# A written order for all engines in the middle of a Strassen MLP, and the first two products of every pair swapped

## Chip, cores and metric

The kernel runs on one core of one Trainium2 chip. The metric is the device time of one execution in microseconds (us), taken as the median of several runs; lower is better.

## What is computed

One layer of a hybrid decoder over 16 meta rows, 1024 prompt rows and 8 x 8 sample rows: two recurrent branches behind one big projection, then a squared-ReLU MLP. What matters here is that nearly all time goes into dense products with 1024-wide activations.

```python
def layer(x, conv_buf, h0, S0, is_prompt, lb, gains, w_in, ...):
    xn = rms_norm(x, gains[0])
    proj = xn @ w_in
...
    mixed = jax.nn.sigmoid(m_a) * (y_a @ w_branch_a) + jax.nn.sigmoid(m_b) * (y_b @ w_branch_b)
    x = x + rms_norm(mixed @ w_out, gains[1])
    hn = rms_norm(x, gains[2])
    ff = jnp.square(jax.nn.relu(hn @ w_up)) @ w_down
    x = x + rms_norm(ff, gains[3])
```

## The kernel before

Every dense product is a 2 x 2 block product in Winograd's form of Strassen's scheme: seven block products in place of eight. A **pair** is one such product: seven weight operands S1, A11, A22, S2, S3, A12, S4 (blocks of the weights and sums of blocks) times seven operands made of the activations. Each operand is held as two f16 tiles, a high part `sh` and a low part `sl`, so that one product is 12 matmuls (4 depth tiles, three combinations of parts, lines 287 to 290). A pair is run twice, once for each half of the columns; one such run of seven products is called a **window** here, c0 and c1 its two columns' halves.

The products of a window accumulate in four PSUM banks b1 to b4. Four products open a bank, three more are added into banks b3, b4 and b1 once the first content has been read out: ACT copies one, DVE adds the next to the copy (that sum is `v`), ACT copies a third (`u`), DVE subtracts. In the kernel before the order is S1 into b4 (ACT copies it, line 1426 in the MLP), S3 into b3 (DVE adds it to v, line 1428), A11 into b1 (ACT copies it, line 1430), S2 into b2 (DVE, line 1432), then A22 onto b3, S4 onto b4, A12 onto b1. So the fifth product, A22, may start only when DVE has read b3 at line 1428.

**Weights of the next pair** are made ready while a pair runs, by the generator `gen_pair` in seven steps (splits): ACT writes `sh` (line 190), DVE writes `sl` (line 191). Sums of blocks are made by DMA: a plain load by SP (line 179) and then an accumulating DMA from the POOL queue onto the same tile `sa` (line 180) give S1; two more accumulating DMAs turn it into S2 (line 222, after the split of S1) and S4 (line 231, after the split of S2). Line 225 turns the tile `ws` with A11 into S3; line 228 (SP) loads A12 over A22; line 161 loads the raw blocks two pairs ahead. There are two `sa` tiles, so the load at line 179 for a later pair waits until S4 of the pair before has been split. The pool `opp` has 11 slots for split operands.

The MLP has 32 pairs: in four groups, four up-projections (`BH`, results squared and split into the f16 tiles `aoh` and `aol` by `up_fin`) and four down-projections (`BA`, results added into `facc` by `dn_fin`). Pairs are numbered 0 to 31 here; pairs 2 to 27 are the **middle**, pairs 0 and 1 (three narrow windows each) the head, pairs 28 to 31 the tail. Before the MLP, the projections and branches use the same scheme through `pair` and `dopair` (line 293).

A scheduler sets the order on each engine from its own estimate of times; each engine then runs its queue strictly in that order. In the MLP TensorE alone runs in the order of the code; ACT, DVE, POOL and SP are in the scheduler's order.

## Time and profile before

| | us |
|---|---|
| median of 3 runs (1943.08 to 1946.82) | 1946.52 |
| the profiled execution | 1943.99 |
| its span, first to last instruction | 1942.2 |
| TensorE busy (92% of the span) | 1782.7 |
| DVE busy (76%) | 1466.5 |
| ACT busy (52%) | 1012.5 |
| middle of the MLP, 1283.2 to 1832.1 | 548.9 |

The span is a chain of stages that TensorE runs through without overlap, so a stage's length and TensorE's waits in it are what counts. Busy shares are averages. Durations of instructions on one engine overlap a little, so the distance between two starts is the time that an instruction costs in a full queue.

### The profile page before, as it was taken

How to read it: one execution, taken by the hardware profiler on the slowest of the kernel's cores; microseconds unless marked ns; L12 is line 12 of the kernel's file. 1: busy time of each engine (PE TensorE's matmuls, PEld its weight loads, DVE VectorE, ACT ScalarE, POOL GpSimd, SP SyncE). 2: the span in 40 equal slices, each digit the busy share in tenths (PEclk: the TensorE clock that was granted, in tenths of full speed). 3: DMA queues.
4: the chain of work that ended last, by engine and by line, in shares of the span. 5: the costliest groups of instructions: out<-in, count | busy, mean ns of one | idle time of the engine just before them, and what ended most of it. 6: DMA issues, size and time to landing. Idle time of an engine off the chain costs nothing. (4 is left out here: it accounts for less than half of the span.)

```text
span 1942.2 us, 43735 instructions
## 1 busy us (share of the span) xinstructions
PE 1782.7 (92%) x17856; PEld 1520.1 (78%) x17856; DVE 1466.5 (76%) x2670; ACT 1012.5 (52%) x2098; POOL 538.3 (28%) x626
## 2 busy tenths in 40 slices
PE   5999999999999999888798898899999889989986
PEld 4888898898878777667677698788888778777776
DVE  7999989788755899877968757976477447645767
ACT  4555555555444787755424344574375236425653
POOL 3511111111222233344623336551211111111132
PEclk9899999999999999989899999999999999999998
DMA  5253332433345444467778632344545445444535
GB/s 178 61 111 84 80 101 68 123 78 90 90 135 146 99 111 111 113 179 223 220 222 241 181 89 70 85 102 105 119 89 114 90 89 101 104 88 100 120 72 162
DMA packets 117337, 230.32 MB, mean 119 GB/s; under 512 B 11152, under 2 KB 45328, under 8 KB 114064
## 3 DMA queue, kind: packets, MB, share of 16 engines
q0 software_dynamic: 45184, 97.28, 25.5%
q1 hardware_dynamic: 62704, 125.24, 20.1%
q10 hardware_dynamic: 9248, 5.02, 1.0%
q8 instruction: 139, 2.28, 0.5%
q14 instruction: 62, 0.51, 0.1%
HBM read 191.43 MB, written 36.06 MB: 117 GB/s over the span
## 5 line engine op out<-in xcount | busy, mean ns | idle before, releaser
L289 PEld LDWEIGHTS <-sh 128*128 128x128 f16 x3920 | 387.5, 99 | 176.5 <-issue 105.7
L287 PEld LDWEIGHTS <-sh 128*128 128x128 f16 x3920 | 388.3, 99 | 79.5 <-issue 4.9
L290 PEld LDWEIGHTS <-sl 128*128 128x128 f16 x3920 | 387.8, 99 | 75.5 <-DVE sl L191 2.3
L287 PE MATMUL q<-aoh,sh 128*128 128x272 f16 (+2 forms) x1008 | 262.5, 270 | 29.5 <-DVE U L1428 26.9
L287 PE MATMUL pd<-tsh,sh 128*128 128x276 f16 (+1 forms) x960 | 272.7, 285 | 13.4 <-DVE gm L347 4.8
L289 PE MATMUL pd<-tsl,sh 128*128 128x276 f16 (+1 forms) x960 | 273.0, 285 | 0.0
L290 PE MATMUL pd<-tsh,sl 128*128 128x276 f16 (+1 forms) x960 | 272.6, 284 | 0.0
L191 DVE SCALAR_TENSOR_TENSOR sl<-sa,sh 128x512 f16<-128x512 f32 x201 | 149.5, 746 | 163.0 <-ACT sh L190 162.8
L287 PE MATMUL q<-hoh,sh 128*128 128x272 f16 (+2 forms) x952 | 256.4, 274 | 12.7 <-DVE U L1428 11.0
L190 ACT ACTIVATE sh<-ws 128x512 f16<-128x512 f32 x288 | 178.6, 626 | 171.3 <-PE q L289 90.1
L290 PE MATMUL q<-aoh,sl 128*128 128x272 f16 (+2 forms) x1008 | 262.5, 270 | 1.8 <-DVE sl L191 1.8
L289 PE MATMUL q<-aol,sh 128*128 128x272 f16 (+2 forms) x1008 | 262.5, 270 | 0.0
L289 PE MATMUL q<-hol,sh 128*128 128x272 f16 (+2 forms) x952 | 256.5, 274 | 0.0
L290 PE MATMUL q<-hoh,sl 128*128 128x272 f16 (+2 forms) x952 | 256.4, 274 | 0.0
L287 PE MATMUL pd<-xh,sh 128*128 128x276 f16 (+1 forms) x776 | 220.0, 283 | 26.0 <-DVE th L341 8.6
L191 DVE SCALAR_TENSOR_TENSOR sl<-ws,sh 128x512 f16<-128x512 f32 x288 | 208.7, 727 | 41.5 <-ACT sh L190 38.8
L190 ACT ACTIVATE sh<-sa 128x512 f16<-128x512 f32 x201 | 125.2, 627 | 202.7 <-DMA sa<-in_w_pr 60.0
L290 PE MATMUL pd<-xh,sl 128*128 128x276 f16 (+1 forms) x776 | 220.3, 284 | 0.0
L289 PE MATMUL pd<-xl,sh 128*128 128x276 f16 (+1 forms) x776 | 220.2, 284 | 0.0
L852 PE MATMUL pd<-sh,xh 128*128 128x128 f16 (+1 forms) x576 | 103.5, 222 | 2.3 <-ACT F L366 2.0
L854 PE MATMUL pd<-sh,xl 128*128 128x128 f16 (+1 forms) x576 | 103.7, 222 | 0.0
L853 PE MATMUL pd<-sl,xh 128*128 128x128 f16 (+1 forms) x576 | 103.5, 222 | 0.0
(332 smaller groups left out, 4234.2 us busy)
## 6 DMA issues: line engine op xcount, KB each, us to landing
sa<-in_w_pr POOLq DMA_DIRECT2D x105, 256.0 KB, 4.2
ws<-in_w_pr SPq DMA_DIRECT2D x35, 512.0 KB, 3.6
sa<-in_w_up POOLq DMA_DIRECT2D x48, 256.0 KB, 4.3
sa<-in_w_dn POOLq DMA_DIRECT2D x48, 256.0 KB, 4.6
sa<-in_w_pr SPq DMA_DIRECT2D x35, 256.0 KB, 3.4
ws<-in_w_pr POOLq DMA_DIRECT2D x35, 256.0 KB, 6.4
ws<-in_w_pr SPq DMA_DIRECT2D x35, 256.0 KB, 4.4
th<-th POOLq DMA_DIRECT2D x16, 544.0 KB, 7.6
```

The costliest lines, as they stand in the source:

```text
L190: ACT.activation(hi, src, AF.Copy, scale=SW)
L191: DVE.scalar_tensor_tensor(lo, src, SW, hi, op0=OP.mult, op1=OP.subtract)
L287: PE.matmul(o, h[:, k, :], bh[:, k, c0:c0 + w], start=first and k == 0, stop=False, skip_group_check=not first)
L289: PE.matmul(o, h[:, k, :], bl[:, k, c0:c0 + w], start=False, stop=False, skip_group_check=not first)
L290: PE.matmul(o, l[:, k, :], bh[:, k, c0:c0 + w], start=False, stop=(k == nk - 1), skip_group_check=not first)
L852: PE.matmul(po, a, wh[:, k % 4, :], start=(k == 0), stop=False)
L853: PE.matmul(po, a, wl[:, k % 4, :], start=False, stop=False)
L854: PE.matmul(po, b, wh[:, k % 4, :], start=False, stop=(k == KT - 1))
```

## The change

Three things change.

- In all pairs the first two products are swapped: S3 into b3 comes first and is the one that ACT copies into v, S1 into b4 comes second and is the one that DVE adds. A22 still goes onto b3 as the fifth product and S4 onto b4 as the sixth.
- In the middle, the order of the code is the order on TensorE, DVE, ACT, POOL and SP (`manual_schedule` over all of them). `up_window` and `dn_window` write it out, product by product. What an up window leaves over (sums of its results and their split into `aoh` and `aol`) is handed on as `rest` and runs behind the first three products of the next window, as `late(0)` to `late(2)`.
- The seven splits of the next pair's weights stand behind fixed products: in c0 behind the second, fourth and sixth, in c1 behind the first, third, fourth and sixth.

In addition the squaring of an up window's results is done in two instructions, and two additions to `facc` in one.

```diff
@@ -291,17 +291,17 @@
                       skip_group_check=not first)
 
     def pair(ops, B, c0, w, s0, s1, tk):
-        t4, t3, t1, t2 = dtags
+        t3, t4, t1, t2 = dtags
         dtags[:] = [t2, t3, t4, t1]
         U = uvp.tile([P, 2, CT], F32, tag="U", name=nm("U"))
         u, v = U[:, 0, :w], U[:, 1, :w]
+        b3 = dtile(t3)[:, :w]
+        prod(b3, ops["S3"], B(5), 4, c0, w, True)
+        ACT.activation(v, b3, AF.Copy)
+        tk(0)
         b4 = dtile(t4)[:, :w]
         prod(b4, ops["S1"], B(3), 4, c0, w, True)
-        ACT.activation(v, b4, AF.Copy)
-        tk(0)
-        b3 = dtile(t3)[:, :w]
-        prod(b3, ops["S3"], B(5), 4, c0, w, True)
-        DVE.tensor_tensor(v, v, b3, op=OP.add)
+        DVE.tensor_tensor(v, v, b4, op=OP.add)
         tk(1)
         b1 = dtile(t1)[:, :w]
         prod(b1, ops["A11"], B(0), 4, c0, w, True)
@@ -1422,10 +1422,10 @@
             if hook:
                 hook(12 * (w / 2400 + 0.0025))
 
+        p(b3, "S3", 5, True)
+        ACT.activation(v, b3[:, :w], AF.Copy)
         p(b4, "S1", 3, True)
-        ACT.activation(v, b4[:, :w], AF.Copy)
-        p(b3, "S3", 5, True)
-        DVE.tensor_tensor(v, v, b3[:, :w], op=OP.add)
+        DVE.tensor_tensor(v, v, b4[:, :w], op=OP.add)
         p(b1, "A11", 0, True)
         ACT.activation(u, b1[:, :w], AF.Copy)
         p(b2, "S2", 4, True)
@@ -1501,19 +1501,130 @@
     facc = fp.tile([P, 2, KT, HW], F32, name="facc")
     mlp["facc"] = facc
 
+
+
+    def up_window(i, ops, c0, w, late, split):
+        b3, b4, b1, b2 = (qbank()[:, :w] for _ in range(4))
+        U = uvp.tile([P, 2, CT], F32, tag="U", name=nm("U"))
+        u, v = U[:, 0, :w], U[:, 1, :w]
+        eb[0] ^= 1
+        e = ep.tile([P, 4, CQ], F32, tag=f"EB{eb[0]}", name=nm("EB"))[:, :, :w]
+        sc = math.sqrt(SA) / KU
+        prod(b3, ops["S3"], BH(5), 4, c0, w, True)
+        ACT.activation(v, b3, AF.Copy)
+        split(0)
+        late(0)
+        prod(b4, ops["S1"], BH(3), 4, c0, w, True)
+        DVE.tensor_tensor(v, v, b4, op=OP.add)
+        late(1)
+        split(1)
+        prod(b1, ops["A11"], BH(0), 4, c0, w, True)
+        ACT.activation(u, b1, AF.Copy)
+        late(2)
+        split(2)
+        prod(b2, ops["S2"], BH(4), 4, c0, w, True)
+        DVE.tensor_tensor(u, b2, u, op=OP.subtract)
+        DVE.tensor_tensor(e[:, 3], u, v, op=OP.subtract)
+        split(3)
+        prod(b3, ops["A22"], BH(6), 4, c0, w, False)
+        DVE.tensor_tensor(e[:, 2], u, b3, op=OP.subtract)
+        ACT.activation(e[:, 2:4], e[:, 2:4], AF.Relu, scale=sc)
+        split(4)
+        prod(b4, ops["S4"], BH(2), 4, c0, w, False)
+        DVE.tensor_tensor(e[:, 0], b4, u, op=OP.subtract)
+        ACT.activation(e[:, 2:4], e[:, 2:4], AF.Square)
+        ACT.activation(e[:, 0], e[:, 0], AF.Relu, scale=sc)
+        split(5)
+        prod(b1, ops["A12"], BH(1), 4, c0, w, False)
+        ACT.activation(e[:, 1], b1, AF.Relu, scale=sc)
+        ACT.activation(e[:, 0:2], e[:, 0:2], AF.Square)
+        split(6)
+        hh, hl_ = aoh[:, :, i, c0:c0 + w], aol[:, :, i, c0:c0 + w]
+        t = [ebuf(n)[:, :544].rearrange("p (s w) -> p s w", s=2)[:, :, :w] for n in range(2)]
+
+        def rest(k):
+            if k == 0:
+                ACT.activation(hh[:, 0:3], e[:, 1:4], AF.Copy)
+                DVE.tensor_tensor(t[0][:, 0], e[:, 1], e[:, 0], op=OP.subtract)
+                DVE.tensor_tensor(t[0][:, 1], e[:, 3], t[0][:, 0], op=OP.add)
+            elif k == 1:
+                ACT.activation(hh[:, 3:5], t[0], AF.Copy)
+                DVE.tensor_tensor(t[1][:, 0], e[:, 3], e[:, 0], op=OP.subtract)
+                DVE.tensor_tensor(t[1][:, 1], t[0][:, 1], e[:, 2], op=OP.subtract)
+                DVE.tensor_tensor(hl_[:, 0:3], e[:, 1:4], hh[:, 0:3], op=OP.subtract)
+            else:
+                ACT.activation(hh[:, 5:7], t[1], AF.Copy)
+                DVE.tensor_tensor(hl_[:, 3:5], t[0], hh[:, 3:5], op=OP.subtract)
+                DVE.tensor_tensor(hl_[:, 5:7], t[1], hh[:, 5:7], op=OP.subtract)
+
+        return rest
+
+    def dn_window(g, o, ops, c0, w, late, split):
...
+        prod(b3, ops["S3"], BA(5), 4, c0, w, True)
+        ACT.activation(v, b3, AF.Copy)
+        split(0)
+        late(0)
+        prod(b4, ops["S1"], BA(3), 4, c0, w, True)
+        DVE.tensor_tensor(v, v, b4, op=OP.add)
+        late(1)
+        split(1)
...
+        if g == 0:
+            DVE.tensor_tensor(f22, u, v, op=OP.subtract)
+        else:
+            DVE.tensor_tensor(f2, f2, u[:, None].to_broadcast([P, 2, w]), op=OP.add)
+            DVE.tensor_tensor(f22, f22, v, op=OP.subtract)
+        split(3)
...
+        return lambda k: None
+
     npair = 8 * NG - 3
-    for q in range(2, npair - 1):
-        g, i = divmod(q, 8)
-        ops = take()
-        for c in range(2):
-            if i < 4:
-                pairc(ops, BH, c * CQ, CQ, up_fin(i))
-            else:
-                pairc(ops, BA, c * CQ, CQ, dn_fin(g, i - 4))
-            if c == 0:
-                wadv(4)
-            else:
-                drain(cur["gen"])
+    PLACES = ((1, 3, 5), (0, 2, 3, 5))
+    with tc.manual_schedule(engines={E.PE, E.DVE, E.Pool, E.Activation, E.SP}):
+        late = lambda k: None
+        for q in range(2, npair - 1):
+            g, i = divmod(q, 8)
+            ops = take()
+            for c in range(2):
+                def split(k):
+                    if k in PLACES[c]:
+                        wadv(1)
+
+                if i < 4:
+                    late = up_window(i, ops, c * CQ, CQ, late, split)
+                else:
+                    late = dn_window(g, i - 4, ops, c * CQ, CQ, late, split)
+            drain(cur["gen"])
+        for k in range(3):
+            late(k)
     hctx.close()
     l1 = sbuf(ctx, "l1", 21)
     l2 = sbuf(ctx, "l2", 2)
```

POOL's queue at pairs 12 and 13 (both down) before: each DMA from this queue stands here with its line; the `sa` and `ws` numbers tell the pairs' tiles apart.

```order
L222 DMA sa_20630<-in_w_dn 128x512
L180 DMA sa_20880<-in_w_dn 128x512
L225 DMA ws_20511<-in_w_dn 128x512
L231 DMA sa_20630<-in_w_dn 128x512
L180 DMA sa_21117<-in_w_dn 128x512
L222 DMA sa_20880<-in_w_dn 128x512
L225 DMA ws_20774<-in_w_dn 128x512
L231 DMA sa_20880<-in_w_dn 128x512
```

The same place in the changed kernel:

```order
L180 DMA sa_20822<-in_w_dn 128x512
L222 DMA sa_20558<-in_w_dn 128x512
L225 DMA ws_20468<-in_w_dn 128x512
L231 DMA sa_20558<-in_w_dn 128x512
L180 DMA sa_21060<-in_w_dn 128x512
L222 DMA sa_20822<-in_w_dn 128x512
L225 DMA ws_20733<-in_w_dn 128x512
L231 DMA sa_20822<-in_w_dn 128x512
```

Before, L222 of one pair stands ahead of L180 of the next pair's sum at pair 12 and behind it at pair 13; now it stands behind it at every pair of the middle.

ACT's queue over the two windows of pair 13 before (L1426 copies v, L1430 copies u, L190 is a split):

```order
L190 ACTIVATE sh_21120<-sa_20880 128x512
L190 ACTIVATE sh_21125<-ws_20774 128x512
L190 ACTIVATE sh_21130<-ws_20774 128x512
L190 ACTIVATE sh_21135<-sa_20880 128x512
L1426 ACTIVATE U_21021<-q_21017 128x272
L1430 ACTIVATE U_21021<-q_21019 128x272
L190 ACTIVATE sh_21240<-ws_20774 128x512
L1426 ACTIVATE U_21144<-q_21140 128x272
L190 ACTIVATE sh_21244<-ws_20774 128x512
L190 ACTIVATE sh_21250<-sa_20880 128x512
L1430 ACTIVATE U_21144<-q_21142 128x272
```

The same windows in the changed kernel (L1569 copies v, L1577 copies u):

```order
L1569 ACTIVATE U_21033<-q_21029 128x272
L190 ACTIVATE sh_21063<-sa_20822 128x512
L1577 ACTIVATE U_21033<-q_21031 128x272
L190 ACTIVATE sh_21096<-ws_20733 128x512
L190 ACTIVATE sh_21128<-ws_20733 128x512
L1569 ACTIVATE U_21150<-q_21146 128x272
L190 ACTIVATE sh_21164<-sa_20822 128x512
L1577 ACTIVATE U_21150<-q_21148 128x272
L190 ACTIVATE sh_21195<-ws_20733 128x512
L190 ACTIVATE sh_21214<-ws_20733 128x512
L190 ACTIVATE sh_21247<-sa_20822 128x512
```

Before, four splits stood in a row, the fourth of them S2, ahead of the copy of v in c0; now the copy of v is ahead, S1 follows it, and S2 comes in c1 behind that window's copy of v.

DVE's queue in c1 of pair 10 (up) in the changed kernel, from the split of S2 on (L1518 adds the second product to v, L1526 reads the fourth, L1548 to L1558 are what the window before left over, L191 is a split):

```order
L191 SCALAR_TENSOR_TENSOR sl_20406<-sa_20028,sh_20405 128x512
L1548 TENSOR_TENSOR ET_20384<-EB_20259 128x272
L1549 TENSOR_TENSOR ET_20384<-EB_20259,ET_20384 128x272
L1518 TENSOR_TENSOR U_20390<-U_20390,q_20387 128x272
L1552 TENSOR_TENSOR ET_20385<-EB_20259 128x272
L1553 TENSOR_TENSOR ET_20385<-ET_20384,EB_20259 128x272
L1554 TENSOR_TENSOR aol<-EB_20259,aoh 128x3x272
L1557 TENSOR_TENSOR aol<-ET_20384,aoh 128x2x272
L1558 TENSOR_TENSOR aol<-ET_20385,aoh 128x2x272
L191 SCALAR_TENSOR_TENSOR sl_20447<-ws_19938,sh_20446 128x512
L1526 TENSOR_TENSOR U_20390<-q_20389,U_20390 128x272
```

The same window before (L1428 adds to v, L1432 reads the fourth product, L1281 and L1288 are leftovers):

```order
L191 SCALAR_TENSOR_TENSOR sl_20504<-ws_19985,sh_20503 128x512
L1428 TENSOR_TENSOR U_20394<-U_20394,q_20391 128x272
L1281 TENSOR_TENSOR ET_20356<-ET_20355,EB_20347 128x272
L1288 TENSOR_TENSOR aol<-EB_20347,aoh 128x3x272
L191 SCALAR_TENSOR_TENSOR sl_20508<-ws_19985,sh_20507 128x512
L1288 TENSOR_TENSOR aol<-ET_20355,aoh 128x2x272
L191 SCALAR_TENSOR_TENSOR sl_20514<-sa_20104,sh_20513 128x512
L1288 TENSOR_TENSOR aol<-ET_20356,aoh 128x2x272
L1432 TENSOR_TENSOR U_20394<-q_20393,U_20394 128x272
L191 SCALAR_TENSOR_TENSOR sl_20634<-sa_20367,sh_20633 128x512
L191 SCALAR_TENSOR_TENSOR sl_20639<-ws_20248,sh_20638 128x512
```

Before, S1 and A11 of the pair after next (`sl_20634`, `sl_20639`) were already split in this window; now the window splits S2, S3, A12 and S4 of the next pair, and the split of S2 stands ahead of the leftovers and of the addition to v.

## Rows read from the trace of the kernel before

**Rows 1.** The page's first lines: span, and TensorE's busy time.
```profile
span 1942.2 us, 43735 instructions
PE 1782.7 (92%) x17856; PEld 1520.1 (78%) x17856; DVE 1466.5 (76%) x2670; ACT 1012.5 (52%) x2098; POOL 538.3 (28%) x626
```

**Rows 2.** Busy time by stage: us, PE, PEld, DVE, ACT, POOL (count), clock, DMA, GB/s.
```profile
90.00:1120.00 1030.00, 964.89 (x9635) 812.15 (x9633) 852.59 (x1361) 563.44 (x1138) 284.87 (x328) 0.98 0.50 134
1283.20:1832.10 548.90, 520.22 (x4372) 432.49 (x4369) 342.87 (x708) 264.90 (x498) 95.83 (x114) 0.98 0.47 102
1832.10:1928.10 96.00, 84.63 (x1050) 76.68 (x1047) 67.78 (x171) 46.94 (x118) 25.83 (x23) 1.00 0.52 130
```

**Rows 3.** The same view: five undisturbed pairs, and the time after a wait.
```profile
1344.00:1440.00 96.00, 96.00 (x831) 81.04 (x829) 52.63 (x103) 42.81 (x82) 15.95 (x19) 1.00 0.50 106
1510.50:1514.00 3.50, 3.50 (x18) 2.35 (x16) 1.92 (x5) 0.00 (x0) 0.40 (x1) 0.51 0.44 75
```

**Rows 4.** TensorE's waits in the middle, 1283.2 to 1832.1: total us, times, longest.
```profile
PE q L287 <- DVE U L1428: 28.6, 17, 3.6
```

**Rows 5.** Timeline at pair 13: start, duration, engine, line; in brackets idle before, releaser.
```profile
1500.25 0.86 POOL L180 DMA_DIRECT2D sa<-in_w_dn  x1 [13.54 <-DVE facc L1473]
1500.79 1.22 POOL L222 DMA_DIRECT2D sa<-in_w_dn  x1
...
1508.39 0.63 ACT L190 ACTIVATE sh<-sa 128x512 f16<-128x512 f32 x1 [8.11 <-DMA sa<-in_w_dn]
1508.93 0.38 ACT L1426 ACTIVATE U<-q 128x272 f32<-128x272 f32 x1
...
1509.05 0.69 DVE L191 SCALAR_TENSOR_TENSOR sl<-sa,sh 128x512 f16<-128x512 f32 x1 [7.17 <-ACT sh L190]
...
1510.14 0.28 PE L287 MATMUL q<-aoh,sh 128*128 128x272 f16 x1 [3.46 <-DVE U L1428]
```

**Rows 6.** Timeline at pair 11, where L222 stands ahead of L180.
```profile
1459.75 0.86 POOL L222 DMA_DIRECT2D sa<-in_w_dn  x1 [13.79 <-DVE sl L191]
1462.28 0.86 POOL L180 DMA_DIRECT2D sa<-in_w_dn  x1 [1.66 <-DMA sa<-in_w_dn]
...
1463.50 0.63 ACT L190 ACTIVATE sh<-sa 128x512 f16<-128x512 f32 x1 [1.73 <-DMA sa<-in_w_dn]
```

**Rows 7.** Timeline at the end of pair 13: DVE's split of S4, SP's load, POOL's sum.
```profile
1520.90 0.69 DVE L191 SCALAR_TENSOR_TENSOR sl<-sa,sh 128x512 f16<-128x512 f32 x1 [0.65 <-ACT sh L190]
...
1521.62 0.38 SPq L179 DMA_DIRECT2D sa<-in_w_up  x1
...
1525.40 0.86 POOL L180 DMA_DIRECT2D sa<-in_w_up  x1 [14.49 <-DVE sl L191]
```

**Rows 8.** Timeline of DVE in c1 of pair 10, a full queue.
```profile
1455.03 1.00 DVE L1288 TENSOR_TENSOR aol<-EB,aoh 128x816 f16<-128x816 f32 x1
1455.95 0.69 DVE L191 SCALAR_TENSOR_TENSOR sl<-ws,sh 128x512 f16<-128x512 f32 x1
1456.55 0.72 DVE L1288 TENSOR_TENSOR aol<-ET,aoh 128x544 f16<-128x544 f32 x1
...
1458.42 0.44 DVE L1432 TENSOR_TENSOR U<-q,U 128x272 f32<-128x272 f32 x1
1458.77 0.69 DVE L191 SCALAR_TENSOR_TENSOR sl<-sa,sh 128x512 f16<-128x512 f32 x1
```

**Rows 9.** Groups of instructions: an up window's first squaring step, busy us, mean ns, idle.
```profile
L1447 ACT ACTIVATE EB<-EB 128x544 f32<-128x544 f32 (+2 forms) x34 | 21.4, 630 | 35.6 <-DVE EB L1446 35.5
```

**Rows 10.** TensorE's waits before 1130, in the head, and in the tail.
```profile
PE pd L287 <- DVE U L304: 15.1, 9, 6.8
...
PE q L287 <- DVE U L1428: 2.2, 3, 1.5
...
PE q L287 <- DVE U L1428: 7.0, 6, 2.5
PE q L287 <- ACT sh L190: 2.6, 2, 1.6
```

30 lines of the change are left out of this document (added).

## The prediction

> **What bounds the kernel now.** I read the page first, then busy time by stage, TensorE's waits by stage, and last the timelines of one bad and one good pair. TensorE is busy for 1782.7 us of a span of 1942.2 [rows 1], and its stages follow one another, so the question is what it waits for in each. The middle of the MLP is 548.9 us long [rows 2]. It holds 26 pairs of 168 matmuls, 4368 in all. In five pairs that nothing disturbs, 829 matmuls take 96.00 us [rows 3], which is 0.1158 us each, 1.39 us for a product of 12, 9.73 us for a window and 19.46 us for a pair. So 4368 matmuls need 505.8 us, and 43.1 us of the middle are lost. The one wait that the trace lists there is on the addition to v at line 1428: 28.6 us in 17 waits, the longest 3.6 [rows 4]. The rest is what follows the long ones: right after the 3.46 us wait of pair 13 the granted clock is 0.51, which is the 1.2 GHz level, for some 3.5 us [rows 3, 5], and 18 matmuls take the time of 30.
>
> The bad pair shows the mechanism [rows 5]. POOL issues L180, the sum for a later pair, and 0.54 us behind it L222, which turns S1 into S2. ACT's next instruction is the split of S2; it sits idle for 8.11 us until that DMA has landed. Behind it in ACT's queue stands the copy of v, behind that on DVE the split's second half and the addition to v, and TensorE's fifth product waits for that addition. In the good pair [rows 6] L222 goes first, is split 3.75 us after its issue, and L180 follows.
>
> **The change, part by part.**
>
> *The written order, copies of v.* In c0 the copy of v now stands ahead of any split, and S2's split has moved to c1, behind the copy of v there. So a late L222 no longer holds up the fifth product: with the swap that product needs only ACT's copy of the first one, and it has three products, 4.2 us, for that. The addition to v is now needed by the sixth product. The chain of [rows 5] (split of S2, copy, addition, product) is cut in all 26 pairs. What it cost was 43.1 us.
>
> *What is late next: the loop through POOL.* L180 now stands ahead of L222 everywhere. L180 waits for SP's load, and that load waits until S4 of the pair before has been split, since there are two `sa` tiles. That closes a loop: load, L180, L222, split of S2, split of S4, next load. Its parts:
> - From the end of S4's split at 1521.59 the load follows at once and L180 3.78 us after the load's issue [rows 7]: 3.8 us.
> - From L180's issue to L222's data. Lower bound: one such DMA alone takes 3.75 us [rows 6], and L222 is issued about 0.9 later, so 4.6. Upper bound: 8.1 us, where three DMAs went off together [rows 5]. The two behind the first cost (8.1 - 3.75) / 2 = 2.2 us each; in the new order the third, L225, waits for the split of A11, two products later. I take 3.75 + 2.2 = 5.9 us.
> - The split of S2 on ACT and DVE, 0.63 + 0.69 and the handover [rows 5]: 1.4 us.
> - From there to the end of S4's split. In an up window DVE's queue holds five sums at 0.35 us, a split of the window's results at 0.92, two at 0.63, the splits of S3 and A12 at 0.60 each and four more sums at 0.35 [rows 8]: 6.5 us; the last of them feeds ACT, which has three steps of squaring, two of them at 0.63 [rows 9] and a shorter one, some 1.4 us, before S4's split, 1.3 us. That makes 9.1 us with a little overlap. In a down window there is little between, and the limit is L231, 0.3 + 3.75, and S4's split, 1.3: 5.4 us.
>
> The loop is 3.8 + 5.9 + 1.4 + 9.1 = 20.2 us in an up pair and 16.5 in a down pair, against TensorE's 19.46. Up pairs fall back by 0.7 us each, down pairs win up to 3.0 back. Falling back costs nothing at first. ACT reaches S2's split about 11.7 us into the pair in any case; in the first up pair after down pairs L180 is issued at about 4.0 and L222 lands at 9.9, so 1.8 us are free. From the second up pair on, S4 having been split at 22.2, L180 comes at 22.2 + 3.8 - 19.46 = 6.5, L222's data at 12.4, then 0.7 later in each pair: 13.1, 13.8. The first product of the next pair needs S3, whose split ends 4.6 us behind that of S2, at 11.7 + 1.4 + 4.6 = 17.7: 1.8 us of room. The fourth up pair uses up 2.1 of it. So each of the three groups of four up pairs ends with a few tenths of waiting. I book 4 us for this and for handovers, 39 us of gain for the middle. No wait stays above 2 us, so I expect no fall of the clock.
>
> Here the notes have another price. The Trainium skill, "DMA: Bandwidth & Descriptors", section "Anatomy of one DMA — SWDGE (gpsimd) path", gives a POOL-issued DMA as a fixed 2.0 us plus its bytes over 436 GB/s, for 256 KB an estimate of 2.6 us; [rows 6] has 3.75 alone. By the page the loop of an up pair would be under 19.46, none of the 4 us would be left, and the forecast would be 1896.
>
> *DVE's and ACT's load.* An up window costs DVE nine sums at 0.35, one at 0.92, two at 0.63 and 3.5 splits at 0.60 [rows 8]: 7.4 of 9.73 us. It is not the bound while it doesn't stand waiting for S2 for more than 2.3 us a window. The split in two squarings is a fraction of a microsecond on ACT, which is half idle (264.90 of 548.9 [rows 2]); no cost.
>
> *The swap outside the middle.* Before 1130 us TensorE waits 15.1 us in 9 waits for the same addition, line 304, the longest 6.8 [rows 10]. The swap gives each one product, 1.4 us, of air: at most 6 waits of under 1.4 in full, and 1.4 from the longer, 8.5 us in all. The scheduler also lays out this part anew from its own estimates, which moves splits and sums past each other on every queue; nothing in the trace of before prices that, so from 8.5 gained to 8 lost, and I take 3 gained. In the head there are 2.2 us in 3 waits, I take 2. In the tail 7.0 us in 6 waits, of which about 5 can go; but S3, the fifth split, is now needed by the first product instead of the second, and the two waits on splits, 2.6 us [rows 10], can each grow by 1.4. I take 2, from 5 gained to 3 lost.
>
> Sum: 39 + 3 + 2 + 2 = 46. The profiled execution took 1943.99 us (span 1942.2), 2.5 under the median; 1943.99 - 46 = 1898, beside the median 1900.5. **I forecast 1900 us.**
>
> **Rivals.**
>
> *The loop is slower than I took it (R1).* If L222 lands 8.1 us behind L180, as at pair 13, the loop of an up pair is 22.4 us, 2.9 over TensorE's. In a group the first up pair is free, the second waits 1.5, the third and fourth 2.9 each, the first down pair 1.6: 8.9, three groups, and 3 for pairs 2 and 3: 28 us left in the middle. Gain 15 + 7, time 1925. For it: that is what the trace measures with this very order of the queue. Against: there three transfers and an SP load went off together; the new places spread them.
>
> *The loop holds every pair (R2), the case on the slow side.* If the DMAs from POOL slow down beside a DVE that never rests, the same loop decides everything from about 9.6 us between L180 and L222's data: then up pairs lose 4.4 us each (14 of them, 62 us less 12 of room) and down pairs, 3.8 + 9.6 + 1.4 + 5.4 = 20.2, start to lose too, and the 50 us of waits in middle and swap are eaten. At 10.5 us it is 63 for up and 20 for down pairs, 1946.5 + 83 - 50 = 1980. Against it: L222 at 1459.75 was issued just behind a stretch in which DVE ran without a gap [rows 8] and took 3.75 us all the same [rows 6]. This is where a rule of the notes speaks against the change: the Trainium skill, "SBUF — State Buffer", section "SBUF: two separate sides", has POOL-issued DMAs starve for descriptors while DVE runs an operation in a two-port mode. The rows named show no sign of it.
>
> *The swap does harm where the scheduler lays out anew (R3).* The middle gains 39, the first 1130 us lose 8 and the tail 3, the head gains 2: 1946.5 - 30 = 1916.
>
> *Nothing changes (R4):* the copy of v waits elsewhere, for instance behind squarings that wait for DVE. ACT's queue ahead of the copy of v then holds S4's split and two squarings, done about 2 us into the pair; the copy is needed at 5.6. I give it 0.02, 1946.
>
> **How the numbers follow.** Forecast 0.65, R1 0.17, R3 0.12, R4 0.02, R2 0.04. The low end takes all of the 43, 8.5 before, 2 in the head and 5 in the tail: 1946.5 - 58.5 = 1888, and I go to 1887. The high end reaches over R3 and to R1's 1925: 1926. Left out are R2, R4 and part of R1. Faster by more than 0.2% (3.9 us, about what a measurement of this kernel can tell from no change) in all but R2 and R4 and a little of R1: 0.94; within 0.2%: 0.02; slower: 0.04.
>
> **What would show it.** In the profile after: the middle between 506 and 515 us long; no wait of TensorE on the line that adds to v above 1 us and none on the fifth product; the granted clock 1.00 throughout the middle; L180 ahead of L222 on POOL with 5 to 7 us from L180's issue to the split of S2; ACT's waits for `sa` 1 to 2 us, growing from the second to the fourth up pair. R1 would show TensorE waiting at the sixth product of c1 or the first of the next pair, in up groups, by 1.5 to 3 us; R2 in down pairs as well. R3 would show in the first 1130 us alone. I am wrong about the mechanism if ACT no longer waits for S2 and TensorE still waits at the fifth product.

## The result, and the profile after

The changed kernel takes 1928.13 us (median of 4 runs, 1922.59 to 1928.96), the kernel before, timed beside it, 1945.80 (1943.08 to 1946.82): a ratio of 0.9907, with a 95% interval of 0.988 to 0.9934. It is faster, as forecast, by 17.7 us instead of 46; 1928 lies 2 us above the range. The profiled execution took 1927.69.

By stage, from the two traces (a stage begins with TensorE's first product in it):

| stage | before | after | difference | forecast |
|---|---|---|---|---|
| ahead of the MLP's head (start of head) | 1231.1 | 1248.2 | +17.1 | -3 |
| head | 52.1 | 51.4 | -0.7 | -2 |
| middle | 548.9 | 513.7 | -35.2 | -39 |
| tail | 96.0 | 98.4 | +2.4 | -2 |

The page's first lines (span; busy time) stand beside [rows 1]: TensorE has as much to do as before, and the span is 16.3 us shorter.

```profile
span 1925.9 us, 43547 instructions
PE 1780.8 (92%) x17856; PEld 1519.6 (79%) x17856; DVE 1472.3 (76%) x2654; ACT 1013.9 (53%) x2126; POOL 558.4 (29%) x626
```

**The middle did what it should.** Busy time by stage, columns as in [rows 2], and all of TensorE's waits in the middle, as in [rows 4]:

```profile
1299.61:1813.35 513.74, 508.12 (x4372) 426.86 (x4370) 342.44 (x687) 263.33 (x523) 95.64 (x114) 1.00 0.49 107
```

```profile
PE q L287 <- DVE U L1518: 3.6, 7, 0.8
PE q L290 <- DVE sl L191: 2.0, 6, 0.3
```

The 28.6 us in 17 waits of [rows 4] have become 3.6 in 7, none over 0.8, all at the sixth product and none at the fifth. The granted clock is 1.00 where it was 0.98. Against 505.8 us without any stall, 7.9 are left.

**The loss is ahead of the MLP, and in one place.** Ahead of the MLP a trace holds 70 windows of 84 matmuls. The products u and g and gates 3 to 7, beside which the chain of the RG-LRU runs on ACT, DVE and POOL, are windows 28 to 53 (counted from 0). The first five of them lose nothing (52.9 us before, 52.2 after), so I cut at the first matmul of windows 33 and 53, and "the section" means that stretch from here on. Ahead of it (the heads and these five windows) the changed kernel is 4.9 us shorter, behind it 2.2. The section itself, before and after:

```profile
656.13:915.60 259.47, 230.61 (x1808) 180.28 (x1806) 228.69 (x315) 176.59 (x301) 103.89 (x114) 0.96 0.54 141
```

```profile
650.64:934.89 284.25, 236.70 (x1808) 182.42 (x1806) 231.71 (x315) 178.16 (x301) 115.81 (x114) 0.93 0.49 130
```

The same 1808 matmuls take 24.8 us more, at a granted clock of 0.93 instead of 0.96. TensorE's waits there, before and after (lines 300, 304 and 308: copy of v, addition to v, copy of u):

```profile
PE pd L287 <- DVE th L341: 8.6, 3, 5.5
PE pd L287 <- DVE gm L347: 4.8, 4, 2.5
...
PE pd L287 <- DVE U L304: 2.4, 2, 1.8
...
PE pd L287 <- ACT U L308: 1.6, 2, 1.0
```

```profile
PE pd L287 <- ACT U L308: 19.5, 8, 3.9
PE pd L287 <- ACT th L405: 7.9, 2, 7.5
PE pd L287 <- DVE U L304: 6.0, 2, 3.3
PE pd L287 <- DVE th L347: 4.3, 1, 4.3
```

The copy of u is not a line that the diff touches. Five of its eight waits stand some 29 us apart, each at A12 in the first half of a pair (2.5, 3.9, 2.9, 3.7, 2.5 us, together 15.4). They stand in windows 36 to 44; at window 35 the delay is 0.3 us, at window 45 it is 19.4 (counting 84 matmuls to a window), so most of the loss is made there. This is ACT's queue at the second of them, and TensorE behind it:

```profile
719.83 0.38 ACT L300 ACTIVATE U<-pd 128x276 f32<-128x276 f32 x1
...
724.40 1.32 ACT L1068 ACTIVATE th<-th,sm 128x1128 f32<-128x1128 f32 x1
725.62 0.65 ACT L381 ACTIVATE et<-gm 128x552 f32<-128x552 f32 x1
726.29 1.28 ACT L1071 ACT_TABLE_LOAD   x1
727.59 1.14 ACT L1071 ACTIVATE th<-th 128x1128 f32<-128x1128 f32 x1
...
731.22 1.31 ACT L1032 ACTIVATE uc<-up,par,cwk 128x1128 f32<-128x1128 f32 x1
732.44 0.21 ACT L1038 ACTIVATE convout<-up 128x24 f32<-128x24 f32 x1
732.56 0.38 ACT L308 ACTIVATE U<-pd 128x276 f32<-128x276 f32 x1
```

```profile
728.70 0.28 PE L289 MATMUL pd<-xl,sh 128*128 128x276 f16 x1
728.82 0.28 PE L290 MATMUL pd<-xh,sl 128*128 128x276 f16 x1
732.99 0.39 PE L287 MATMUL pd<-xh,sh 128*128 128x276 f16 x1 [3.89 <-ACT U L308]
733.17 0.44 PE L289 MATMUL pd<-xl,sh 128*128 128x276 f16 x1
733.40 0.44 PE L290 MATMUL pd<-xh,sl 128*128 128x276 f16 x1
```

Between the copies of v and u ACT works through 12 us of the RG-LRU, of results and of splits, with a single gap of 0.51 us. TensorE waits 3.89 us, and afterwards its matmuls come 0.23 us apart instead of 0.12, at a granted clock of 0.50 (the third number from the end of this row), the 1.2 GHz level, as after the wait in [rows 5]:

```profile
733.00:736.50 3.50, 3.01 (x13) 1.84 (x13) 3.50 (x4) 0.40 (x1) 0.00 (x0) 0.50 0.34 61
```

Why does the copy of u hurt now? The scheduler sets TensorE's order here too, and the order in which it let the products of one pair begin has changed (p, a, b: second half of the previous pair, first and second half of this one; shown are windows 39 to 41):

```
before   a.S1 a.A11 p.S3 a.S2 a.S4 a.A12 p.A22 | b.S1 b.S2 b.A11 a.S3 b.S4 b.A12 (a.A22 follows)
after    a.S3 a.S2 p.S1 a.S1 a.A22 p.S4 a.S4 a.A11 a.A12 | b.S2 b.S3 b.A11 b.A22 b.A12 (b.S1 follows)
```

Before, in windows 37 to 45, every half leaves S3 and A22 over for the next half, A11 comes early, and at least two products, mostly three in a first half, lie between A11 and A12, in which ACT copies u. After, first halves leave nothing over and A11 stands directly ahead of A12 on the same bank: TensorE has to stand still until u is copied. From window 48 on neither kernel carries anything over. What makes the scheduler do this is what most of the experiments are about.

### The profile page after: what moved, and what is told of

Its sections match the earlier page's. It is cut to its first block, busy times and chain, and to the rows that moved or that the text cites. A ratio compares the mean times of both kernels' runs of the same rounds, so it can differ in the third digit from the quotient of the medians.

```text
span 1925.9 us, 43547 instructions
## 1 busy us (share of the span) xinstructions
PE 1780.8 (92%) x17856; PEld 1519.6 (79%) x17856; DVE 1472.3 (76%) x2654; ACT 1013.9 (53%) x2126; POOL 558.4 (29%) x626
## 5 line engine op out<-in xcount | busy, mean ns | idle before, releaser
L191 DVE SCALAR_TENSOR_TENSOR sl<-ws,sh 128x512 f16<-128x512 f32 x288 | 210.2, 733 | 63.3 <-ACT sh L190 62.6
L287 PE MATMUL pd<-xh,sh 128*128 128x276 f16 (+1 forms) x776 | 222.3, 287 | 36.2 <-ACT U L308 19.5
L191 DVE SCALAR_TENSOR_TENSOR sl<-sa,sh 128x512 f16<-128x512 f32 x201 | 151.1, 754 | 133.0 <-ACT sh L190 131.8
L190 ACT ACTIVATE sh<-ws 128x512 f16<-128x512 f32 x288 | 173.8, 622 | 92.5 <-PE pd L289 63.3
L190 ACT ACTIVATE sh<-sa 128x512 f16<-128x512 f32 x201 | 124.7, 623 | 124.3 <-DMA sa<-in_w_pr 57.1
```

The costliest lines, as they stand in the source:

```text
L190: ACT.activation(hi, src, AF.Copy, scale=SW)
L191: DVE.scalar_tensor_tensor(lo, src, SW, hi, op0=OP.mult, op1=OP.subtract)
L287: PE.matmul(o, h[:, k, :], bh[:, k, c0:c0 + w], start=first and k == 0, stop=False, skip_group_check=not first)
```

## The experiments

### Is it the swap in `pair`, and where?

Four kernels: `pair` put back, the rest as changed (e1); `pair` swapped in the kernel before (e2); the swap only in the RG-LRU section (e3); everywhere but there (e4), the last two by a switch around the first two products that is set ahead of window 28 and behind window 53.

```diff
@@ pair (e1: as before; e2: the reverse, in the kernel before; e3, e4: chosen by section)
-        t3, t4, t1, t2 = dtags
+        t4, t3, t1, t2 = dtags
-        prod(b3, ops["S3"], B(5), 4, c0, w, True)
-        ACT.activation(v, b3, AF.Copy)
+        prod(b4, ops["S1"], B(3), 4, c0, w, True)
+        ACT.activation(v, b4, AF.Copy)
...
```

> The changed kernel with only the helper `pair` put back (S1 first, S3 second, as in the kernel before); the written middle and the swap in `pairc` stay. In the trace of the changed kernel the last product ahead of the MLP ends 15 us later than before (1134.3 against 1119.3) and the MLP's head starts 17.1 us later, while the middle is 35.2 us shorter. Theory A, the swap in `pair` makes that loss by itself: the last product ahead of the MLP goes back to 1119 to 1121, the middle keeps its 513.7, and the time is 1928 - 17 = 1911 (1908 to 1914). Rival B, the written middle changes what the scheduler does ahead of it, so that the loss is not the swap's: the end ahead of the MLP stays at about 1134 and the time at 1928.

> The kernel before with nothing changed but `pair` (S3 first, S1 second); the MLP is as it was. Theory A: the last product ahead of the MLP at about 1134 instead of 1119, and 1946 + 17 = 1963 (1959 to 1966). Rival B (the loss comes with the written middle): 1943 to 1946, the end ahead of the MLP at 1116 to 1120. The prediction's own step said 1943.

> The changed kernel with the swap in `pair` only from the RG-LRU section on (the u and g products and gates 3 to 7) up to the start of the y products; the heads and gates 0 to 2, and the y products, run in the old order. In the trace of the changed kernel the lead over the kernel before is 4.8 us at window 33 (the heads gain a little) and turns to a delay of about 19 us by window 49. Theory A1, the loss is made where it shows, in the RG-LRU section: no gain in the heads, the same delay of 20 to 24 us in the section, and 1911 + 22 = 1933 (1928 to 1938). Rival A2, the loss is handed over by what the swap does earlier, in the heads (a background that is left over, a rotated buffer): no delay here, 1908 to 1914.

> The mirror of the run with the swap in the RG-LRU section only: the swap in `pair` everywhere but there. Theory A1 (the loss is made in the RG-LRU section): the heads keep their gain of 2 to 5 us, the section costs nothing, and the time is 1928 - 22 = 1906 (1903 to 1911). Rival A2 (the loss is handed over from the heads): the end ahead of the MLP stays near 1134 and the time at 1924 to 1930.

| kernel | median us | ratio to before (95%) | RG-LRU section us |
|---|---|---|---|
| e1, `pair` as before | 1913.42 | 0.9831 (0.9814 to 0.9849) | 260.1 |
| e2, only `pair` swapped | 1962.70 | 1.0090 (1.0068 to 1.0111) | 284.1 |
| e3, swap in the section only | 1935.67 | 0.9948 (0.9933 to 0.9964) | 284.4 |
| e4, swap everywhere but there | 1900.05 | 0.9764 (0.9740 to 0.9788) | 259.7 |

All four came out as theory A and A1 had it (e4 3 us better than its range): the written middle has no part in the loss, the swap makes it by itself, and all of it in the RG-LRU section, by 24.1 to 24.6 us in each pair of kernels. Outside the section the swap gains a little. Everything else from the first window to the MLP's head takes 871.5 to 880.3 us in the 16 kernels with the swap or one of its variants (below) there, and 880.8, 888.3, 880.5 and 881.0 in the four without: 8 us by the means, 6 if the 888.3 of e1 is left out. By the medians e4 is 13.4 us faster than e1, and the changed kernel 7.5 faster than e3, so the size of this gain is known only roughly. How far single executions scatter shows e1, whose products ahead of the MLP end 5.5 us later than before (1124.8 against 1119.3) with the instructions of all engines in the very same order up to there; so a difference of a few us in one place of one trace says nothing, and only the 20 and more in the section do.

### What about the swap does it?

First, three guesses that fell or said little, each on the changed kernel or on e4 (whose section is in the old order). The mirror image, S1 first but S4 fifth and A22 sixth (e8, in the section alone; e12, everywhere ahead of the MLP); u copied by DVE (e9); six splits instead of four in a pair's first half (e10).

```diff
@@ pair, in the section (e8) or everywhere (e12), with S1 first
-        prod(b3, ops["A22"], B(6), 4, c0, w, False)
-        s1.both(c0, w, (u, b3), (u, v))
         prod(b4, ops["S4"], B(2), 4, c0, w, False)
         s0.one(1, c0, w, b4, u)
+        prod(b3, ops["A22"], B(6), 4, c0, w, False)
+        s1.both(c0, w, (u, b3), (u, v))
@@ pair, in the section (e9)
-        ACT.activation(u, b1, AF.Copy)
+        DVE.tensor_copy(u, b1)
@@ dopair, in the section (e10)
-                if (c == 0 and i in (1, 2, 4, 6)) or c == 1:
+                if (c == 0 and i in (0, 1, 2, 4, 5, 6)) or c == 1:
```

> The same base, but in the RG-LRU section the mirror image of the swap: S1 first and S3 second as in the kernel before, and instead of them the fifth and the sixth product change places (S4 fifth, on the bank that ACT copied; A22 sixth, on the bank that DVE added). The fifth product gets the same extra time between its bank's last reader and its first matmul as in the changed kernel, without S3's weights coming first. Theory H (that the extra time makes the scheduler lay the section out anew, and the new layout is the loss): the section costs 15 to 25 us, time 1915 to 1925. Rival I (what costs is S3 as first product, whose weights are the fifth of seven splits): section at most 4 us, time 1898 to 1904.

> The changed kernel with `pair` as the mirror image everywhere ahead of the MLP: S1 first and S3 second as before, S4 fifth and A22 sixth. With `pair` as before everywhere the time is 1913, with the swap outside the RG-LRU section and the old order or the mirror within it 1900. Theory O (the 13 us between these come from the extra time that the fifth product gets outside the section, and the mirror gives the same): 1897 to 1904. Rival P (they come from the order of S3 and S1, or from a chance layout): 1909 to 1917.

> The changed kernel with one edit: in the RG-LRU section the copy of u (line 300 plus 8 of the changed kernel, ACT, 0.38 us) is done by DVE. In the trace of the changed kernel TensorE waits 21.4 us in 9 places for that copy, which stands on ACT behind the RG-LRU's exponential, table loads, square root and convolution. Theory J (that place in ACT's queue is the loss): the waits go, the section loses 16 to 22 us less, time 1906 to 1913. Rival K (the queues are full in these stretches, and the wait moves to the next evacuation on ACT or onto DVE): time 1920 to 1932.

> The changed kernel, and in the RG-LRU section the splits of the next pair's weights stand earlier in the code: six in a pair's first half, behind every product but the fourth, instead of four, so that S3's split (the fifth) stands two products earlier. Theory M (the section loses because S3, the first product now, has its weights so late that the scheduler plans the pair late and puts other work of ACT and DVE ahead of it): the section loses at most 12 instead of 24.8, time 1905 to 1916. Rival N (the place of S3's split is not the reason): 1922 to 1934.

e8 took 1900.31 us (0.9774, 0.9753 to 0.9794), section 258.6; e12 1900.74 (0.9759, 0.9735 to 0.9784), section 257.9. Rival I and theory O hold by their numbers, but the mirror is a weaker test than I meant it to be: in the section the scheduler gives it the same order of products as the kernel before, since it leaves S3 and A22 over in any case (windows 36 to 44 are in the very same order). e9 took 1927.32 (0.9911, 0.9881 to 0.9942), section 287.3, and the wait moved to DVE, as rival K said:

```profile
PE pd L287 <- DVE U L311: 21.4, 6, 5.7
```

Line 311 is that kernel's copy of u. So neither ACT nor DVE, both with full queues, copies u in time. e10 took 1927.11 (0.9902, 0.9873 to 0.9932), section 284.6: rival N, moving S3's split two products ahead does not help, and TensorE's order of products in windows 36 to 44 stays that of the changed kernel.

Next, the order of products and the banks. S3 first with S4 fifth (e13). Changed kernel with A22 and S4 held back until A11 has been issued (e16). The line that hands the banks on, changed so that A11 takes over the first product's bank (e14, changed kernel) or the second's (e15, S1 first, on e4).

```diff
@@ pair, e14 everywhere; e15 in the section, in its branch with S1 first
-        dtags[:] = [t2, t3, t4, t1]
+        dtags[:] = [t2, t4, t3, t1]
@@ pair, in the section (e16); the same for S4
-        prod(b3, ops["A22"], B(6), 4, c0, w, False)
+        with tc.issue_after(a11.ins):
+            prod(b3, ops["A22"], B(6), 4, c0, w, False)
```

> The kernel with the swap in `pair` everywhere but in the RG-LRU section (1900 us), and in that section S3 first and S1 second as in the changed kernel, but S4 fifth and A22 sixth, so that the fifth product stands on the bank that DVE adds, without extra time. It is the fourth case of the section: S1 first with A22 fifth 0 us, S3 first with A22 fifth +24.8, S1 first with S4 fifth about -0.5, and this one. Theory I (S3 ahead of S1 is what costs): +18 to +30, time 1918 to 1930. Rival L (only S3 first together with the extra time costs, because then the addition of v may come late): 0 to 6, time 1898 to 1906.

> The changed kernel with one order forced in the RG-LRU section: TensorE may issue a pair's fifth and sixth products (A22, S4) only behind its A11, so that A11 and A12 are never neighbours. Banks and everything else stay. Theory S (the neighbourhood of A11 and A12, with the copy of u between them, is the loss): the five waits of together 15.4 us go, time 1908 to 1917. Rival T (A11 stands late because its bank is late; forced ahead, TensorE waits for the bank instead): 1922 to 1936.

> The changed kernel with one line of `pair` changed, the one that hands the four PSUM banks on to the next half: t3 and t4 change places in it, so that A11 of the next half takes over the bank of the first product (now S3's, finished fifth) instead of the second's (now S1's, finished sixth), as it does in the kernel before by product slot. In the changed kernel's instructions the scheduler has put A11 directly ahead of A12, on the same bank, in the first half of five u pairs; A12 then has to wait for ACT's copy of u, and the five long waits for that copy (2.5, 3.9, 2.9, 3.7, 2.5 us, together 15.4) are at these places. Theory Q (the bank that A11 takes over is released too late, so the scheduler defers A11): the section loses at most 10 instead of 24.8 us, time 1905 to 1914. Rival R (A11 is deferred for another reason, or the loss comes from the gates): 1922 to 1934.

> The kernel with the swap in `pair` everywhere but in the RG-LRU section (1900 us), which has S1 first there; in that section the banks are handed on with t3 and t4 exchanged, so that A11 takes over the bank of the second product (here S3's). It is the reverse of the run that changes the hand-over in the changed kernel. Theory Q (what costs is that A11 inherits the bank of the second product): the section costs 8 to 25 us, time 1908 to 1925. Rival U (only S3 first costs, whichever way the banks go): 1896 to 1904.

| kernel | median us | ratio to before (95%) | section us |
|---|---|---|---|
| e13, S3 first, S4 fifth | 1931.48 | 0.9920 (0.9893 to 0.9946) | 286.1 |
| e16, A11 held ahead of A22 and S4 | 1928.24 | 0.9917 (0.9892 to 0.9942) | 287.2 |
| e14, S3 first, banks handed on otherwise | 1921.66 | 0.9866 (0.9832 to 0.9899) | 280.7 |
| e15, S1 first, banks handed on otherwise | 1922.78 | 0.9873 (0.9838 to 0.9908) | 279.6 |

e13 is theory I's (1.5 us above its range): the extra time for the fifth product doesn't matter, though here too the scheduler gives windows 36 to 44 the changed kernel's order. e16 is rival T's. In the first halves A11 and A12 now stand two products apart, and TensorE waits less for the copy of u (its line 311, beside 19.5 us and 3.9 above), but more for two of DVE's instructions (lines 315 and 406; 0.3 and 1.0 us for the same two in the changed kernel):

```profile
PE pd L287 <- ACT U L311: 10.9, 7, 2.2
...
PE pd L287 <- DVE U L315: 7.6, 6, 1.7
PE pd L287 <- DVE up L406: 7.5, 5, 3.4
```

The same time is lost in other waits, so the neighbourhood looks like the form of the loss and not its cause. That is not settled: the forced order is a new layout with waits of its own, and in most of the second halves a single product stands between A11 and A12, as in the changed kernel. In each of the slow orders of this study some window from 36 to 44 has one product or none between the two, in the fast ones never fewer than two. e14 missed both ranges (theory Q by 8 us, the rival by less than one): the section is 3.5 us shorter, and still 21 too long. e15 fits theory Q: with S1 first, and nothing but another hand-over of banks, the section loses 20 us. What e14 and e15 share is in the order of products: neither carries any product from one half into the next within the section.

That left the roles: who is copied into v and who is added to it. Two kernels cross them with the written order. e20 has S1 first and the old banks, but v begins with S3; e22 has S3 written first, but v begins with S1, and each product is on its old bank.

```diff
@@ pair, e20 (against the kernel before)
         prod(b4, ops["S1"], B(3), 4, c0, w, True)
-        ACT.activation(v, b4, AF.Copy)
         tk(0)
         prod(b3, ops["S3"], B(5), 4, c0, w, True)
-        DVE.tensor_tensor(v, v, b3, op=OP.add)
+        ACT.activation(v, b3, AF.Copy)
+        DVE.tensor_tensor(v, v, b4, op=OP.add)
@@ pair, e22 (against the changed kernel)
-        dtags[:] = [t2, t3, t4, t1]
+        dtags[:] = [t3, t2, t4, t1]
         prod(b3, ops["S3"], B(5), 4, c0, w, True)
-        ACT.activation(v, b3, AF.Copy)
         tk(0)
         prod(b4, ops["S1"], B(3), 4, c0, w, True)
-        DVE.tensor_tensor(v, v, b4, op=OP.add)
+        ACT.activation(v, b4, AF.Copy)
+        DVE.tensor_tensor(v, v, b3, op=OP.add)
```

> The changed kernel with `pair` as in the kernel before in the order of its products (S1 first) and in its banks; of the swap it keeps only the roles of the two evacuations: ACT copies S3's bank into v, DVE then adds S1's. Theory X (the loss comes from v starting with S3, whose weights come late in the row of splits: S1's bank can't be let go before S3's copy, while in the kernel before S1 is copied at once and S3 with its bank may run one half late): the RG-LRU section costs 18 to 28 us though S1 is first, time 1918 to 1932. Rival Y (the order in which the two products are written costs): section 0 to 5, time 1896 to 1908.

> The converse: the changed kernel with S3 written first and S1 second in `pair`, but with the roles as in the kernel before (ACT copies S1's bank, DVE adds S3's) and each product on the bank that it has there (S3's bank stays S3's from half to half). Theory X: the section costs at most 5 us, time 1896 to 1908. Rival Y (S3 written first costs): section 18 to 28 us, time 1918 to 1932.

e20 took 1928.44 us (0.9927, 0.9908 to 0.9947), e22 1903.13 (0.9801, 0.9770 to 0.9833). The section's row of e20 and then of e22:

```profile
650.18:939.19 289.01, 236.22 (x1808) 181.92 (x1806) 227.38 (x315) 177.97 (x302) 122.36 (x114) 0.94 0.49 130
```

```profile
653.62:913.05 259.43, 227.11 (x1809) 178.22 (x1806) 227.29 (x311) 175.04 (x299) 104.35 (x113) 0.97 0.52 138
```

Theory X holds both ways: 289.0 us with S1 first, 259.4 with S3 written first (e20's loss in the section, 29.5 us, is 1.5 above its range). The products of one pair, as laid out:

```
e20      a.S1 p.S3 a.S2 p.A22 p.S4 a.S3 a.A11 a.A22 a.A12 a.S4 | b.S1 b.S2 b.A11 b.A12 (b.S3, b.A22, b.S4 follow)
e22      a.S1 a.A11 p.S3 a.S2 a.S4 a.A12 p.A22 | b.S1 b.S2 b.A11 a.S3 b.S4 b.A12 (a.A22 follows)
```

e22, with S3 first in the code, has the order of the kernel before in these windows. e20 carries three products over and is slow all the same, so carrying alone is not what makes the old layout fast. Over all 20 traces: ten kernels in which v begins with S1 and the banks go as before have sections of 257.6 to 261.9 us; ten in which either is changed have 279.6 to 289.0, and none lies between. These are not twenty cases: in windows 36 to 44 there are only eight orders of products. Nine of the fast ten share that of the kernel before (e22 has one of its own), and five of the slow ten share that of the changed kernel. The crossing of roles, banks and written order rests on one kernel each: e20, e15 and e22.

### What carries the middle, and what is left in it?

e6 is e4 with S1 first and copied in the written middle; e7 is the kernel before with only `pairc` swapped; e5 is e4 with L222 ahead of L180 on POOL in the middle; e17 is e12 with S2's split one place later.

```diff
@@ up_window, dn_window (e6); the reverse in pairc of the kernel before (e7)
-        prod(b3, ops["S3"], BH(5), 4, c0, w, True)
-        ACT.activation(v, b3, AF.Copy)
+        prod(b4, ops["S1"], BH(3), 4, c0, w, True)
+        ACT.activation(v, b4, AF.Copy)
...
@@ sum_load and gen_pair, in the middle (e5)
-            nc.gpsimd.dma_start(q, src[:, 1], accum_op=OP.add)
...
             nc.gpsimd.dma_start(q, src[:, 2], accum_op=OP.add)
+            nc.gpsimd.dma_start(q2, src2[:, 1], accum_op=OP.add)
@@ the middle (e17)
-    PLACES = ((1, 3, 5), (0, 2, 3, 5))
+    PLACES = ((1, 3, 5), (1, 2, 3, 5))
```

> The same base (swap in `pair` everywhere but in the RG-LRU section), and in the written middle alone the first two products in the old order: S1 first and copied by ACT, S3 second and added by DVE, the fifth product again on the bank that DVE reads. The places of splits and leftovers stay. Theory F (the written order carries the middle's gain, since the addition of v then stands right behind its product): middle 510 to 518, time 1896 to 1903. Rival G (the swap carries it): the fifth product waits for the addition of v again, 1 us or more in each of some 17 places as before, middle 530 to 549, time 1916 to 1934.

> The kernel before with nothing changed but the first two products in `pairc`: the scheduler still sets ACT's, DVE's and POOL's order in the middle. With the run that has the written order and S1 first this makes four cases of the middle: 548.9 us (neither), 513.7 (both), 517.9 (written order alone), and this one (swap alone). Theory F (the written order carries the gain, the swap only a little): middle 535 to 552, time 1931 to 1949. Rival G (the swap alone would have done it, since 28.6 us of the middle's waits are on the addition of v, and the fifth product no longer waits for it): middle 515 to 528, time 1911 to 1924.

> The kernel with the swap in `pair` everywhere but in the RG-LRU section (1900 us), and in the written middle one thing more: on the POOL queue the second addition into the pair's own sum (line 222 of before) is issued ahead of the first addition of the next pair's sum (line 180 of before). The middle of the base lasts 514.8 us for 26 pairs of 19.46 = 506.0; what is left are stalls of under 1 us at the sixth product of the second half and at the third matmul of the next pair's first product. Theory D (the loop of additions over the POOL queue makes them, 4 us or more of them): the middle falls to 506 to 510 and the time to 1893 to 1896. Rival E (the splits' fixed places make them, whatever comes from the queue): middle 514 to 516, time 1899 to 1901.

> The kernel with the mirror image of the swap everywhere ahead of the MLP (1901 us, middle 514.0), and in the written middle the split of S2 in the second half one place later, behind the second product instead of the first, so that on DVE it no longer stands ahead of the addition of v. What is left of stalls in the middle is 0.4 to 1.0 us at the sixth product of the second half in the up pairs, which waits for that addition, and 0.5 us at the next pair's first product. Theory V (the split ahead of the addition makes the first kind, some 6 us): middle 507 to 510, time 1893 to 1898. Rival W (DVE has too much to do in the up pairs, and the lateness only moves on): middle 513 to 518, time 1899 to 1905.

| the middle, us | scheduler's order | written order |
|---|---|---|
| S1 copied, S3 added | 548.9 (before) | 517.9 (e6) |
| S3 copied, S1 added | 533.1 (e7) | 513.7 (after) |

The times are 1909.85 us for e6 (0.9823, 0.9802 to 0.9844) and 1926.91 for e7 (0.9891, 0.9853 to 0.9929). For the middle's length e6 is theory F's, its time 7 us above what was expected, half of it in the tail; e7 lies between the two ranges. The written order alone is worth 31.0 us, the swap alone 15.8, both 35.2: they cut the same chain, at two places. Under the scheduler the swap moves what is left of the wait to the other reader, the copy of v (line 1426), as this row of e7 shows:

```profile
PE q L287 <- ACT U L1426: 21.0, 13, 2.8
```

e5 took 1901.45 (0.9783, 0.9760 to 0.9806), its middle 516.8 against 514.7 in e4: nearest to rival E (0.8 us above its range), the order on POOL is not what is left. e17 took 1895.11 (0.9738, 0.9711 to 0.9764), and its middle is theory V's (1 us better than its range), with nothing left: its row by stage, and for DVE the stretch around the addition to v (line 1518) in c1 of pair 11, first of the changed kernel, then of e17.

```profile
1274.88:1780.84 505.96, 505.96 (x4372) 427.40 (x4370) 343.74 (x688) 260.83 (x523) 96.07 (x114) 1.00 0.50 109
```

```profile
1492.40 0.69 DVE L191 SCALAR_TENSOR_TENSOR sl<-sa,sh 128x512 f16<-128x512 f32 x1 [1.08 <-ACT sh L190]
1493.01 0.43 DVE L1548 TENSOR_TENSOR ET<-EB 128x272 f32<-128x272 f32 x1
1493.47 0.44 DVE L1549 TENSOR_TENSOR ET<-EB,ET 128x272 f32<-128x272 f32 x1
1493.83 0.43 DVE L1518 TENSOR_TENSOR U<-U,q 128x272 f32<-128x272 f32 x1
```

```profile
1462.99 0.69 DVE L191 SCALAR_TENSOR_TENSOR sl<-ws,sh 128x512 f16<-128x512 f32 x1 [1.90 <-ACT sh L190]
1463.96 0.44 DVE L1548 TENSOR_TENSOR ET<-EB 128x272 f32<-128x272 f32 x1 [0.28 <-ACT EB L1540]
1464.44 0.44 DVE L1549 TENSOR_TENSOR ET<-EB,ET 128x272 f32<-128x272 f32 x1
1464.80 0.43 DVE L1518 TENSOR_TENSOR U<-U,q 128x272 f32<-128x272 f32 x1
...
1466.77 0.69 DVE L191 SCALAR_TENSOR_TENSOR sl<-sa,sh 128x512 f16<-128x512 f32 x1
```

TensorE at the sixth product of that window in the changed kernel:

```profile
1493.23 0.28 PE L290 MATMUL q<-hoh,sl 128*128 128x272 f16 x1
1494.32 0.28 PE L287 MATMUL q<-hoh,sh 128*128 128x272 f16 x1 [0.81 <-DVE U L1518]
```

In the changed kernel the low part of S2 (1492.40, from `sa`) makes DVE wait 1.08 us for its high part on ACT, runs, and only then come two leftovers and the addition, 1.0 us too late for the sixth product. In e17 it stands behind them (1466.77), the addition ends 1.5 us ahead of that product's start at 1466.70, and TensorE is busy for all of 505.96 us: 26 pairs at the 19.46 of [rows 3], with no wait on any row. e17 is the fastest kernel of the study, 51 us under the kernel before and 33 under the changed one.

## Why the prediction was wrong

**The middle: right in the mechanism, 39 forecast, 35.2 measured.** The chain of [rows 5] is cut, the signs named are there: 513.7 us is inside 506 to 515, nothing waits at the fifth product, no wait is over 1 us, and the clock holds at 1.00.

**What is late next: right that a few us stay (4 booked, 7.9 left), wrong about what holds them.** The loop through POOL was computed from the fact that L180 stands ahead of L222. e5 turns the two round and gains nothing. What the loop was to bring came about when forecast: in the second to fourth up pair of the second group (pairs 9 to 11) L222's data landed 12.0, 12.8 and 14.3 us into the pair, where 12.4, 13.1 and 13.8 were forecast. What failed is "ACT reaches S2's split about 11.7 us into the pair in any case". It did so in pair 8 (11.6), and then fell back, 13.1, 14.6 and 15.6 us into pairs 9 to 11, later than the data each time. So ACT never waited for `sa` in an up pair; its 17 such waits, 27.1 us in all, lie in down pairs. What held the addition back was the split's low part on DVE, a cost that the step on DVE's load had dismissed because DVE is not full: it is not, but ACT and DVE wait for each other in turn, and what stands behind pays. At pair 11 of the changed kernel ACT waits for DVE, then DVE for ACT, and then DVE 1.08 us more, as shown above:

```profile
1488.40 0.66 ACT L1531 ACTIVATE EB<-EB 128x544 f32<-128x544 f32 x1 [3.10 <-DVE EB L1530]
1490.62 0.69 DVE L191 SCALAR_TENSOR_TENSOR sl<-ws,sh 128x512 f16<-128x512 f32 x1 [1.90 <-ACT sh L190]
```

The price of the Trainium skill, "DMA: Bandwidth & Descriptors", section "Anatomy of one DMA — SWDGE (gpsimd) path", under which nothing would have been left, is not tested by this, since the loop never held TensorE up. Its estimate of 2.6 us stands against 3.75 measured [rows 6].

**The swap outside the middle: this is the step that failed.** I priced it by the waits for the addition at line 304 [rows 10], allowed from 8.5 gained to 8 lost, and took 3 gained; the stretch ahead of the MLP's head lost 17.1. Behind the section the priced wait did shrink, from 12.6 us to 7.4:

```profile
PE pd L287 <- DVE U L304: 12.6, 7, 6.8
```

```profile
PE pd L287 <- DVE U L304: 7.4, 2, 6.4
```

The copy of v (line 300) took 3.9 us of that back (2.7 to 6.6). The 4.9 us gained ahead of the section are not what was priced: there is no wait on line 304 there in either kernel. The rest, 24.8 us lost in the section, lies beyond the lower bound. That bound had no row behind it. The text itself said that nothing in the trace prices a new layout, and then put a number there that mirrors the gain. The trace did hold a sign: in windows 37 to 45 of the kernel before, S3 and A22 of each half run in the next one, which one sees in TensorE's queue once it is read by products. The swap makes v, and with it S1's bank, wait for S3, and by product it hands the banks on otherwise too. The roles alone cost 29 us in the section (e20), another hand-over of the banks alone 20 (e15).

**Head and tail: too small to settle.** The head gained 0.7 of 2. In the tail the waits for the addition fell from 7.0 us [rows 10] to 1.4, as priced, and the waits on splits grew, from 4.4 us (the 2.6 of [rows 10] and the first line here) to 8.7 (the other two):

```profile
PE q L290 <- DVE sl L191: 1.8, 2, 1.4
```

```profile
PE q L287 <- ACT sh L190: 6.1, 3, 3.3
PE q L290 <- DVE sl L191: 2.6, 4, 1.8
```

But the tail is 94.0 to 99.4 us long in kernels with the swap in the tail, and 96.0 and 95.8 in the two without, so its +2.4 is within what executions differ by.

**The rivals.** R1 and R2, the loop, did not come about. (R1's sum has a slip: three times 8.9 and 3 make 29.7 us, not 28, which puts its time at 1926, at the very end of the range.) R3 had the right mechanism and place, at 0.12 and with 8 us in place of 17.

**What stays open.** Shown is that the swap makes the loss, in the section, and that with the written order as before a change of roles alone (e20) or of one hand-over of banks alone (e15) makes it too, while the written order alone (e22) does not. The layout with S3 and A22 carried into the next half goes with the fast section in every kernel here. Which property of a layout costs the time is open, and so is whether the old one is a lucky one: the six other orders of products all cost 20 us or more, but they come from a handful of sets of roles and banks. Why the scheduler lets S3 lag there was only argued, from its being the fifth of seven splits; moving that split two products ahead (e10) changed nothing. That the mirror image costs nothing follows from its layout.

## What to carry to other kernels

An edit that exchanges two equal-looking operations also exchanges which buffer is let go early and which chain may lag; before pricing it, look for a chain that the order lets run late (here products that run in the next half) and ask who will now wait for it. Where a scheduler lays out the neighbourhood anew, apply the edit only where the order is written by hand, or measure it by section; here the swap was worth 15.8 us in one place and cost 24.8 in another. Once an order is written by hand, the last stalls come from what stands ahead of the awaited instruction in its own queue, and moving one such step by one place can be worth more than the transfer behind it: e17 took the last 8.1 us out of the middle of its base e12 (514.0 to 506.0), e5 on the transfers nothing.
